# Two more Strassen pairs in each of four feed-forward blocks, and the sums they read as a task of their own

## The chip, the core and the metric

The kernel runs on one core of one Trainium2 chip. What counts is the device time of one execution, in microseconds (us). The four engines that matter here are PE (TensorE, matmuls and transpositions), DVE (VectorE), ACT (ScalarE) and POOL (GpSimd); SP issues the loads. Each engine works through its own instructions in a fixed order.

## The reference

Two stacked blocks on a sequence of 512 rows with 1024 features. What is touched here is the SwiGLU feed-forward layer (inner width 2816), which stands four times in the first part of the model, each time followed by a scaled residual and a LayerNorm:

```python
def swiglu_ffn(x, wi, wo):
    gate, up = jnp.split(x @ wi, 2, axis=-1)
    return (jax.nn.silu(gate) * up) @ wo
```

All of it is in float32. Mixers of several kinds, attention and two further feed-forward blocks stand between and behind; the change does not touch their code.

## The kernel before, in words

**Precision.** A float32 product is made of three matmuls of a shorter type: each operand is split into a high part (`xh`, `wh`, made by ACT as a rounded copy) and a low part (`xl`, `wl`, made by DVE as the difference), and PE adds `wh.xh + wh.xl + wl.xh` (`mm3`; its matmuls are all on line 319 of the profile, transpositions on line 324). Operations of the other engines go through a wrapper and all show line 55, so they are told apart by their tiles.

**A feed-forward block** (`ffn_block1`, called four times: blocks 1 to 4 below). The 22 pairs of gate and up slabs of 128 columns go in three parts of 6, 8 and 8 pairs (`PARTS`); after each part a down-projection (`down`, tile `mg` in the first part) adds what the part gives. The four products of pairs 0 and 1 are made by `gemm_first`, tile `mf`, k by k while x is being completed. A *plain* pair from then on is two products of 8 k-steps x 3 matmuls of 512 columns, tile `m`: 48 matmuls. After a pair, ACT makes the sigmoid part `sg`, DVE `hf`, ACT `hh`, DVE `hl` (`unit`).

**A Strassen pair** (class `Fast`, weights in class `Pair`). A pair's product is a 2 x 2 block product: the two weight slabs by the two halves of the inner dimension, against the halves of x's features and of its columns. In the Winograd form it takes seven products of half the size instead of eight: A11, S2, A12, S3, S1, A22, S4, in that order, each 4 k-steps x 3 matmuls of 256 columns, 84 matmuls. A11 and A12 read x itself; S4's product reads x too; S2, S3, S1 and A22 read four *combinations* T1 to T4 of x. The weights S1 to S4 are sums of raw slabs (`ws`, `wr`) that DVE makes. The low parts of S1 and S2 do not go over DVE: ACT writes minus the high part, and a DMA of GpSimd's queue adds the raw value (`wl<-ws`). The results are put together on DVE from the parts of PSUM.

**The combinations** (class `Combos`). First the eight sums `ys[k] = xh + xl` (tiles `y`, 128x512, DVE); from these, in four steps of k, two tiles `ta` and `tb` by four DVE operations of 256 columns; ACT's `th` and DVE's `tl` split each. The `y` are later also the accumulators of the down-projection.

**The order of the work.** `Sched` holds a model of the engines' times while the program is written out: tasks (generators) are kept in a list with due times, and `wait`, `upto` and `pump` run them where they are due. A task yields a due time (`pace`: not over 2 us ahead of DVE), or a condition. The compiler's scheduler then also sets the order in which each engine's instructions stand. That order, once built, is fixed: an engine does not pass an operation that waits.

**Before the change**, which pairs are Strassen pairs is the tuple `FAST`: pairs 4 to 7, 9, 10, 12 to 15, 17, 18, 20, 21. The eight sums are emitted behind `gemm_first` and the first units, and the combinations are then a task (`cb.make`). Pairs 2 and 3 are plain. Block 1 starts with `load_start`: x is read in eight pieces, transposed by PE (tile `xT`) in two halves of k, and split, all before the first matmul of `gemm_first`.

Of the kernel before, what the change touches and what calls it, by code (L numbers as in the profile page):

```python
# [14 lines left out]
ALU = mybir.AluOpType  # L15
AX = mybir.AxisListType
PSUM = bass.MemoryType.PSUM
P = 128
NT = 512
KD = 8  # L20
# [499 lines left out]
HALF = (slice(0, 256), slice(256, 512))  # L520
ALPHA = 4.0 ** 0.25
PARTS = ((0, 6), (6, 8), (14, 8))
FAST = (4, 5, 6, 7, 9, 10, 12, 13, 14, 15, 17, 18, 20, 21)
RAW1, HL1 = 6, 7


# [72 lines left out]
def load_start(g, x, X0, n=4):  # L599

    g.preload(AF.Silu)
    ts, raw = {}, {}
    for hf in range(2):
        for t in range(4):
            a = ts[t, hf] = g.f("xs")
            g.nc.sync.dma_start(a, x[t * P:(t + 1) * P, hf * NT:(hf + 1) * NT])
        for j in range(n):
            a = raw[j, hf] = g.f("wr")
            g.wq[j][0](a.rearrange("p (k c) -> p k c", k=4), 4 * hf, 4)
    for j in range(n):  # L610
        g.whl_t[j] = []
    for hf in range(2):
        for o in range(4):
            k = 4 * hf + o
            ps = g.psum("xT")
            for t in range(4):
                g.tr(ps[:, t * P:(t + 1) * P], ts[t, hf][:, o * P:(o + 1) * P])
            g.split_x(X0.h[k], X0.l[k], ps)
        for j in range(n):
            hi, lo = g.f("wh", F32R), g.f("wl", F32R)  # L620
            g.split_x(hi, lo, raw[j, hf])
            g.whl_t[j] += [(hi[:, k * P:k * P + P], lo[:, k * P:k * P + P]) for k in range(4)]
    g.wi_dma = g.wi_hi = g.wi_split = n
    X0.ready = [KD, KD]


def gemm_first(g, xs, n, by_half=True):

    w = [g.slab(0) for _ in range(n)]
    g.acq_main(n)  # L630
    ps = [g.psum("mf") for _ in range(n)]
    for hf, c in enumerate(HALF if by_half else (slice(0, NT),)):
        for k in range(KD):
            g.s.wait(lambda: xs.ready[hf] > k)
            g.s.upto(*xs(k), w[0][k][1])
            for j in range(n):
                g.mm3(ps[j][:, c], w[j][k], xs(k, c), k == 0, k == KD - 1)
            if k % 2 and (hf or not by_half):
                g.split_ahead()
            g.s.pump()  # L640
    g.slab_done(n)
    return ps
# [107 lines left out]
def down(g, xs_of, kt):  # L750

    yield from head(g, xs_of, kt, 2)
    for m in range(2, KD):
        yield m, gemm_tile(g, xs_of, kt)
# [60 lines left out]
class Combos:  # L815
# [3 lines left out]
    def __init__(self, g, xs, ys):  # L819
        self.g, self.xs, self.ys = g, xs, ys  # L820
        self.t = {}
        self.n = 0

    def make(self):
        g = self.g
        TT = g.nc.vector.tensor_tensor
        a, b = HALF
        for k in range(4):
            lo, hi = self.ys[k], self.ys[4 + k]
            s, u = g.f("ta"), g.f("tb")  # L830
            TT(s[:, a], lo[:, b], lo[:, a], ALU.subtract)
            TT(s[:, b], hi[:, b], s[:, a], ALU.subtract)
            yield g.pace()
            TT(u[:, a], hi[:, b], lo[:, b], ALU.subtract)
            TT(u[:, b], hi[:, a], s[:, b], ALU.subtract)
            yield g.pace()
            for nm, t in (("s", s), ("u", u)):
                h, l = g.f("th", F32R), g.f("tl", F32R)
                g.split_x(h, l, t)
                self.t[nm, k] = (h, l)  # L840
            self.n = k + 1
            yield g.pace()
        self.ys = None
# [71 lines left out]
            g.rel()  # L915


def ffn_block1(g, xs, gv, bv, hook=None, into=None, by_half=True, fast=()):

    nc = g.nc  # L920
    ys = [g.f("y") for _ in range(KD)]
    st = Stats(g, True)
    pipe = Pipe()
    for pi, (k0, n) in enumerate(PARTS):
        hs = {}

        def unit(j, pg, pu):
            sg, hf = g.f("sg"), g.f("hf")
            nc.scalar.activation(sg, pg(), AF.Silu)
            g.rel()  # L930
            yield True
            nc.vector.scalar_tensor_tensor(hf, sg, 0.5, pu(), ALU.mult, ALU.mult)
            g.rel()
            hh, hl = g.f("hh", F32R), g.f("hl", F32R)
            nc.scalar.activation(hh, hf, AF.Copy)
            yield True
            nc.vector.tensor_tensor(hl, hf, hh, ALU.subtract)
            hs[j] = (hh, hl)

        def unit_fast(j, e):  # L940
            sg, hf = e.c1, e.c2
            nc.scalar.activation(sg, sg, AF.Silu)
            yield True
            nc.vector.scalar_tensor_tensor(hf, sg, 0.5, hf, ALU.mult, ALU.mult)
            hh, hl = g.f("hh", F32R), g.f("hl", F32R)
            nc.scalar.activation(hh, hf, AF.Copy)
            yield True
            nc.vector.tensor_tensor(hl, hf, hh, ALU.subtract)
            hs[j] = (hh, hl)

        j = k0
        if pi == 0:
            ps = gemm_first(g, xs, 4, by_half)
            for i in range(2):
                pipe.add(unit(i, lambda: ps[2 * i], lambda: ps[2 * i + 1]))
                pipe.step()
            j = 2
            for k in range(KD):
                nc.vector.tensor_tensor(ys[k], xs.h[k], xs.l[k], ALU.add)
            g.raw_lim, g.hl_lim, g.ahead = RAW1, HL1, 2  # L960
            cb = Combos(g, xs, ys)
            if fast:
                g.s.spawn(cb.make())
        open_ = {}
        for j, nm in pair_order(range(j, k0 + n), fast):
            if nm is None:
                ps = [gemm_tile(g, xs)]
                pipe.add(unit(j, lambda: ps[0], lambda: ps[1]))
                ps.append(gemm_tile(g, xs))
                pipe.step()  # L970
                continue
            g.s.wait(lambda: cb.n == 4)
            if j not in open_:
                open_[j] = Fast(g, cb)
            e = open_[j]
            e.step(nm)
            if nm == "S4":
                pipe.add(unit_fast(j, e))
                del open_[j]
        pipe.drain()  # L980
        if pi == len(PARTS) - 1:
            g.raw_lim, g.ahead = 0, 1
        of = lambda k, c=slice(0, NT): (hs[k0 + k][0][:, c], hs[k0 + k][1][:, c])
        if pi == 0:
            for m, ps in down(g, of, n):
                nc.vector.scalar_tensor_tensor(ys[m], ys[m], ALPHA, ps, ALU.mult, ALU.add)
                g.rel()
        elif pi == 1:
            for m, ps in down(g, of, n):
                nc.vector.tensor_tensor(ys[m], ys[m], ps, ALU.add)  # L990
                g.rel()
        else:
            xn = []

            def evac(m, ps, c):
                nc.vector.tensor_tensor(ys[m][:, c], ys[m][:, c], ps, ALU.add)

            def finish(hf):
                if not xn:
                    xn.append(into() if into else X(g, "x"))  # L1000
                if into:
                    return xn[0].ln_half(st, ys, hf, gv, bv)
                return ln_half(g, st, ys, hf, gv, bv, xn[0])

            out_proj_ln(g, ys, of, n, 4, evac, st, finish, head(g, of, n, 2))
        if hook and pi == 0:
            hook()
    return xn[0]
# [1877 lines left out]
def kernel(ctx: ExitStack, tc: tile.TileContext, d, out: bass.AP):  # L2886
    g = G(ctx, tc)
    x0 = X(g, "x")
# [17 lines left out]
    def first_setups():  # L2906
        yield lambda: g.vec_done
        setup_even(g, d)
        yield 20000.0
        setup_blk2(g, d)  # L2910

    plan_ffn(g, d["ffn1_wi"][0], d["ffn1_wo"][0], fast=FAST)
    plan_even(g, d["ev_w_in"][0], d["ev_w_out"][0])
    plan_ffn(g, d["ffn2_wi"][0], d["ffn2_wo"][0], fast=FAST)
    plan_ffn(g, d["ffn1_wi"][1], d["ffn1_wo"][1], fast=FAST)
    plan_odd(g, d["od_w_in"][0], d["od_w_out"][0], lambda l: plan_mem(g, d["w_mem_kv_2"][l]))
    plan_ffn(g, d["ffn2_wi"][1], d["ffn2_wo"][1], fast=FAST)
    for l in range(2):
        plan_attn(g, d, l)
        plan_ffn2(g, d, l)  # L2920
    load_start(g, d["x"][0], x0)

    ln = lambda l, i: (v[f"ln_g{l}{i}"], v[f"ln_b{l}{i}"])
    def man(n):
# [5 lines left out]
        return tc.manual_schedule(engines=e) if e != set() else contextlib.nullcontext()  # L2930

    with man("f"):
        x = ffn_block1(g, x0, *ln(0, 0), hook=lambda: g.s.spawn(first_setups()), by_half=False, fast=FAST)
    with man("even"):
        x = even_block(g, x, d, *ln(0, 1))
    with man("f"):
        x = ffn_block1(g, x, *ln(0, 2), fast=FAST)
        x = ffn_block1(g, x, *ln(1, 0), hook=lambda: setup_odd(g, d), fast=FAST)
    mkv, mhl = [], ([], [])
    with man("odd"):  # L2940
        x = odd_block(g, x, d, *ln(1, 1), mem_norm(g, d["mem_2"][0], v["mem_norm_g"], *mhl),
                      lambda l: mkv.append(mem_kv(g, *mhl)))
    g.hl_bufs = HB1
    with man("f3"):
        rx = ffn_block1(g, x, *ln(1, 2),
                            into=lambda: RX(g, [g.f("x") for _ in range(KD)], v["g_pre_mix0"]), fast=FAST)
# [42 lines left out]
```

## Time and profile before

| what | value |
|---|---|
| times of three runs | 3631.16, 3628.79, 3620.95 us (median 3628.79) |
| the profiled execution's own time | 3618.88 us |
| its span, first to last instruction | 3616.9 us |
| mean granted TensorE clock | 0.991 |
| PE busy | 3548.0 us, 98% of the span, 21720 instructions |
| DVE busy | 2412.3 us, 67% |
| ACT busy | 1641.5 us, 45% |
| POOL busy | 423.0 us, 12% |

The time is that of a whole execution, the span that of its instructions. A row of the timeline gives the start, the busy time, engine, line, operation, output and inputs with their shapes, and in brackets the idle time before it and what ended it. The first row of a run of n like operations shows the busy time of all n. A matmul's own duration contains the part in which the next already runs, so the pitch from one to the next is the cost.

### The profile page before, as it was taken

The numbers are of one execution on the slowest core, as the hardware profiler recorded it, in microseconds if no ns is written. First come the engines' busy times: TensorE is split into PE (matmuls) and PEld (weight loads), VectorE is DVE, ScalarE is ACT, GpSimd is POOL, SyncE is SP. The second block draws the span as 40 slices with busy tenths as digits, with TensorE's granted clock in tenths as the row PEclk, the third lists the DMA queues.
The fourth block names the chain that finished last, engine by engine and source line by source line (L and its number), as shares of the span: only waits on it lengthen the run. The fifth ranks groups of instructions, "written<-read, shape, count | busy, mean of one in ns | idle before, by whom it ended". The sixth has DMA issues, their size and how long they took to land.

```text
span 3616.9 us, 57977 instructions
## 1 busy us (share of the span) xinstructions
PE 3548.0 (98%) x21720; PEld 3024.1 (84%) x21720; DVE 2412.3 (67%) x4499; ACT 1641.5 (45%) x3169; POOL 423.0 (12%) x615
## 2 busy tenths in 40 slices
PE   9999999999999999988999999999999999999999
PEld 7889868898989997667888988788888987888888
DVE  6666968775776577776865675557656745467755
ACT  5444764444444456533543454435434444354433
POOL 0102003000210021011100210021000110120001
PEclk9999999999999999998999999999999999999999
DMA  5555322454445441113354533232333252333331
GB/s 150 132 128 124 88 59 81 107 135 117 110 120 129 112 106 48 37 53 88 85 132 122 124 116 110 88 111 62 106 101 93 75 153 73 96 88 104 92 90 53
DMA packets 631243, 361.52 MB, mean 100 GB/s; under 512 B 27025, under 2 KB 609842, under 8 KB 630962
## 3 DMA queue, kind: packets, MB, share of 16 engines
q1 hardware_dynamic: 612018, 324.81, 31.2%
q0 software_dynamic: 16128, 29.37, 5.0%
q8 instruction: 170, 2.79, 0.3%
q10 hardware_dynamic: 2816, 3.64, 0.3%
q14 instruction: 111, 0.91, 0.1%
HBM read 323.65 MB, written 4.74 MB: 91 GB/s over the span
## 4 chain that ended last, share of the span: by engine, by line
PE 45%; DVE 3%; issue 1%; DMA 1%; ACT 1%; POOL 0%; DVEq 0%; ACTq 0%; POOLq 0%
PE m L319 33%; PE mg L319 3%; PE mf L319 2%; PE tk L319 2%; PE br L319 2%; PE mh L319 1%; DVE rm_t L55 0%; DMA wl<-ws 0%; PE naS L319 0%; PE naO L319 0%; PE dO L319 0%; DVE x L55 0%; PE naT L324 0%; PE st L319 0%; DVE xgl L55 0%
## 5 line engine op out<-in xcount | busy, mean ns | idle before, releaser
L55 DVE TENSOR_TENSOR wl<-wr,wh 128x512 fp32r<-128x512 f32 (+2 forms) x1264 | 864.9, 724 | 236.7 <-ACT wh L55 213.5
L55 ACT ACTIVATE wh<-wr 128x512 fp32r<-128x512 f32 (+2 forms) x1264 | 696.4, 608 | 118.6 <-PE m L319 44.5
L319 PE MATMUL m<-xgh,wh 128*128 128x512 f32 x1184 | 471.2, 398 | 1.2 <-DVE dmx L55 1.2
L319 PE MATMUL m<-xgh,wl 128*128 128x512 f32 x1184 | 467.2, 395 | 0.0
L319 PE MATMUL m<-xgl,wh 128*128 128x512 f32 x1184 | 467.2, 395 | 0.0
L319 PE MATMUL m<-xh,wh 128*128 128x512 f32 (+1 forms) x1320 | 455.4, 345 | 0.1
L319 PE MATMUL m<-xh,wl 128*128 128x512 f32 (+1 forms) x1320 | 446.8, 339 | 2.9 <-DVE wl L55 2.9
L319 PE MATMUL m<-xl,wh 128*128 128x512 f32 (+1 forms) x1320 | 446.3, 338 | 0.0
L319 PEld LDWEIGHTS m<-xh,wh 128*128 128x128 f32 x1320 | 249.4, 189 | 38.2 <-issue 8.4
L319 PEld LDWEIGHTS m<-xh,wl 128*128 128x128 f32 x1320 | 249.6, 189 | 32.9 <-DVE wl L55 4.0
L319 PEld LDWEIGHTS m<-xl,wh 128*128 128x128 f32 x1320 | 249.8, 189 | 28.9 <-issue 1.7
L319 PEld LDWEIGHTS m<-xgh,wh 128*128 128x128 f32 x1184 | 222.7, 188 | 57.1 <-issue 4.8
L319 PEld LDWEIGHTS m<-xgh,wl 128*128 128x128 f32 x1184 | 222.7, 188 | 52.3 <-issue 0.2
L319 PEld LDWEIGHTS m<-xgl,wh 128*128 128x128 f32 x1184 | 222.8, 188 | 50.2 <-issue 0.2
L319 PE MATMUL m<-th,wl 128*128 128x256 f32 x896 | 252.3, 282 | 6.5 <-DMA wl<-ws 6.3
L319 PE MATMUL m<-tl,wh 128*128 128x256 f32 x896 | 251.0, 281 | 0.0
L319 PE MATMUL m<-th,wh 128*128 128x256 f32 x896 | 250.1, 281 | 0.0
L319 PE MATMUL m<-hh,wh 128*128 128x512 f32 x600 | 236.5, 394 | 0.0
L319 PE MATMUL m<-hl,wh 128*128 128x512 f32 x600 | 236.4, 394 | 0.0
L319 PE MATMUL m<-hh,wl 128*128 128x512 f32 x600 | 236.2, 394 | 0.0
L55 POOL DMA_DIRECT2D wl<-ws x112 | 96.2, 859 | 1109.6 <-ACT wl L55 781.7
L319 PEld LDWEIGHTS m<-th,wl 128*128 128x128 f32 x896 | 168.6, 188 | 8.3 <-DMA wl<-ws 8.1
(577 smaller groups left out, 7484.4 us busy)
## 6 DMA issues: line engine op xcount, KB each, us to landing
wr<-in_ffn_wi_dram SPq DMA_DIRECT2D x352, 256.0 KB
wr<-in_w_up_dram SPq DMA_DIRECT2D x176, 256.0 KB
wr<-in_ffn_wo_dram SPq DMA_DIRECT2D x160, 256.0 KB
wr<-in_w_in_dram SPq DMA_DIRECT2D x152, 256.0 KB
wl<-ws POOLq DMA_DIRECT2D x112, 256.0 KB, 3.9
wr<-in_w_down_dram SPq DMA_DIRECT2D x80, 256.0 KB
wr<-in_od_w_in_dram SPq DMA_DIRECT2D x50, 256.0 KB
wr<-in_ev_w_in_dram SPq DMA_DIRECT2D x48, 256.0 KB
```

The source lines that it names most:

```text
L55: r = fn(*a, **kw)
L319: return self.nc.tensor.matmul(out, lhsT, rhs, start=start, stop=stop, **kw)
```

## The change

1. `FAST` has 16 pairs instead of 14: pairs 2 and 3 are added, and in the second part 7 to 10 take the place of 6, 7, 9, 10 (pair 8 in, pair 6 out). It holds for all four blocks.
2. The eight sums are the beginning of a new task, `Combos.sums`, which is started ahead of `gemm_first`, waits until x is complete, writes the sums one by one at DVE's pace, and goes on with `make`.
3. `load_start` transposes and splits only the first half of x, and returns a function for the second half; `gemm_first` calls that in block 1 at k = 2.
4. Ahead of the first down-projection stands a wait in the emission, until all four combinations are written.

The first lines of the diff that say so:

```diff
-FAST = (4, 5, 6, 7, 9, 10, 12, 13, 14, 15, 17, 18, 20, 21)
+FAST = (2, 3, 4, 5, 7, 8, 9, 10, 12, 13, 14, 15, 17, 18, 20, 21)
...
-    for hf in range(2):
+
+    def half(hf):
         for o in range(4):
             k = 4 * hf + o
             ps = g.psum("xT")
...
-            g.whl_t[j] += [(hi[:, k * P:k * P + P], lo[:, k * P:k * P + P]) for k in range(4)]
+            parts[j] += [(hi[:, k * P:k * P + P], lo[:, k * P:k * P + P]) for k in range(4)]
+        X0.ready = [4 + 4 * hf] * 2
...
-    X0.ready = [KD, KD]
+    half(0)
+    return lambda: half(1)
...
         for k in range(KD):
+            if second and k == 2:
+                second()
             g.s.wait(lambda: xs.ready[hf] > k)
...
+    def sums(self):
+
+        g, xs, ys = self.g, self.xs, self.ys
+        yield lambda: min(xs.ready) == KD
+        for k in range(KD):
+            g.nc.vector.tensor_tensor(ys[k], xs.h[k], xs.l[k], ALU.add)
+            yield g.pace()
+        yield from self.make()
...
         if pi == 0:
-            ps = gemm_first(g, xs, 4, by_half)
+            cb = Combos(g, xs, ys)
+            if fast:
+                g.s.spawn(cb.sums())
+            ps = gemm_first(g, xs, 4, by_half, second)
...
-            for k in range(KD):
-                nc.vector.tensor_tensor(ys[k], xs.h[k], xs.l[k], ALU.add)
             g.raw_lim, g.hl_lim, g.ahead = RAW1, HL1, 2
-            cb = Combos(g, xs, ys)
-            if fast:
-                g.s.spawn(cb.make())
...
         if pi == 0:
+            g.s.wait(lambda: cb.n == 4)
             for m, ps in down(g, of, n):
```

The built program has 19666 instructions on PE instead of 19378 (36 more for each of eight pairs), 4468 instead of 4380 on DVE, 3023 instead of 2975 on ACT, 16 more on POOL, and as many on SP.

**DVE, block 2, behind the first product.** Before, the two `hf` (which read `mf` and the sigmoid `sg`) come first, then the sums and the combinations, with weights' low parts and the next units between:

```order
L55 SCALAR_TENSOR_TENSOR hf_6719<-sg_6718,mf_6414 128x512
L55 TENSOR_TENSOR hl_6723<-hf_6719,hh_6722 128x512
L55 SCALAR_TENSOR_TENSOR hf_6727<-sg_6726,mf_6416 128x512
L55 TENSOR_TENSOR y_6403<-xh_6224,xl_6232 128x512
...
L55 TENSOR_TENSOR y_6410<-xh_6231,xl_6239 128x512
L55 TENSOR_TENSOR ta_6746<-y_6403 128x256
L55 TENSOR_TENSOR hl_6731<-hf_6727,hh_6730 128x512
L55 TENSOR_TENSOR ta_6746<-y_6407,ta_6746 128x256
L55 TENSOR_TENSOR wl_6780<-wr_6640,wh_6778 128x512
```

Now the last of four sums stands ahead of the first `hf`, four stand behind the second, and the four steps of combinations follow without a break; weights' low parts come behind the last `tl`:

```order
L55 TENSOR_TENSOR y_6534<-xh_6355,xl_6363 128x512
L55 TENSOR_TENSOR wr_6228<-wr_6228,ws_6724 128x512
L55 SCALAR_TENSOR_TENSOR hf_6829<-sg_6828,mf_6542 128x512
L55 TENSOR_TENSOR hl_6833<-hf_6829,hh_6832 128x512
L55 SCALAR_TENSOR_TENSOR hf_6837<-sg_6836,mf_6544 128x512
L55 TENSOR_TENSOR y_6535<-xh_6356,xl_6364 128x512
...
L55 TENSOR_TENSOR ta_6847<-y_6531 128x256
L55 TENSOR_TENSOR tb_6848<-y_6535,y_6531 128x256
L55 TENSOR_TENSOR ta_6847<-y_6535,ta_6847 128x256
L55 TENSOR_TENSOR tb_6848<-y_6535,ta_6847 128x256
L55 TENSOR_TENSOR tl_6854<-ta_6847,th_6853 128x512
...
L55 TENSOR_TENSOR tl_6900<-tb_6890,th_6899 128x512
```

Blocks 3 and 4 read alike, with seven sums ahead of the first `hf` in block 3.

**PE, block 2, behind the first product.** Before, the first product is followed by a plain pair:

```order
L319 MATMUL mf_6416<-xl_6239,wh_6092 128x256
L319 MATMUL mf_6416<-xh_6231,wl_6096 128x256
L319 MATMUL m_6745<-xl_6232,wh_6591 128x512
L319 MATMUL m_6745<-xh_6224,wl_6595 128x512
L319 MATMUL m_6745<-xh_6225,wh_6591 128x512
```

Now it is followed by A11 (tile `m_6903`) and A12 (`m_6965`) of pair 2, 12 matmuls each, of which the last two stand first here; then S2 and S3 alternate, six matmuls for each step of the combinations; then two of S1 (`m_7010`), whose third reads the low part that comes by DMA:

```order
L319 MATMUL m_6965<-xl_6367,wh_6761 128x256
L319 MATMUL m_6965<-xh_6359,wl_6794 128x256
L319 MATMUL m_6903<-th_6853,wh_6727 128x256
L319 MATMUL m_6965<-th_6857,wh_6797 128x256
L319 MATMUL m_6903<-tl_6854,wh_6727 128x256
...
L319 MATMUL m_6965<-th_6899,wl_6825 128x256
L319 MATMUL m_7010<-th_6853,wh_6916 128x256
L319 MATMUL m_7010<-tl_6854,wh_6916 128x256
L319 MATMUL m_7048<-xh_6356,wh_6926 128x256
```

Seven further matmuls (six of S4, one of A11 of pair 3) stand between these and S1's third.

**DVE, block 1.** The second half of x (`xl_97` to `xl_100`) stood right behind the first product's first four low parts; now four operations on pair 2's weights stand ahead of it:

```order
L55 TENSOR_TENSOR wl_177<-wr_118,wh_176 128x512
L55 TENSOR_TENSOR wl_228<-wr_190,wh_226 128x512
L55 TENSOR_TENSOR ws_230<-wr_192,wr_194 128x512
L55 TENSOR_TENSOR ws_231<-ws_230,wr_190 128x512
L55 TENSOR_TENSOR wr_192<-wr_190,wr_192 128x512
L55 TENSOR_TENSOR xl_97<-xT_236,xh_89 128x512
```

Before, `xl_97` stood directly behind `wl_177`.

## Rows read from the trace of the kernel before

**Rows 1.** The core's span and its mean granted clock.
```profile
core 0: 3616.9 us, clock 0.991
```

**Rows 2.** Windows: length, PE, PEld, DVE, ACT, POOL busy (x), PEclk, DMA, GB/s.
```profile
992.00:1014.30 22.30, 22.30 (x98) 18.09 (x98) 18.37 (x33) 10.53 (x19) 1.74 (x2) 1.00 0.23 53
1014.30:1036.70 22.40, 20.68 (x169) 20.00 (x168) 20.43 (x42) 13.05 (x26) 1.72 (x2) 1.00 0.41 101
15.90:39.10 23.20, 23.20 (x98) 18.80 (x97) 9.38 (x15) 9.63 (x17) 0.00 (x0) 1.00 0.71 186
```

**Rows 3.** The chain that ended last: start, length, what.
```profile
1790.84 4.77 DMA wl<-ws
...
2480.78 18.97 PE mf L319 x160
...
2667.50 11.15 PE mg L319 x48
```

**Rows 4.** PE's waits: in total, times, longest.
```profile
PE m L319 <- DMA wl<-ws: 6.3, 7, 1.7
```

**Rows 5.** Timeline of DVE in block 3, behind the first product.
```profile
993.05 0.69 DVE L55 SCALAR_TENSOR_TENSOR hf<-sg,mf 128x512 f32<-128x512 f32 x1 [2.44 <-ACT sg L55]
...
995.64 4.90 DVE L55 TENSOR_TENSOR y<-xh,xl 128x512 f32<-128x512 f32 x8
...
1015.01 0.42 DVE L55 TENSOR_TENSOR ta<-y 128x256 f32<-128x256 f32 x1
...
1018.01 0.42 DVE L55 TENSOR_TENSOR ta<-y 128x256 f32<-128x256 f32 x1
```

**Rows 6.** Timeline of DVE: the first hf of blocks 2 and 4.
```profile
634.60 0.69 DVE L55 SCALAR_TENSOR_TENSOR hf<-sg,mf 128x512 f32<-128x512 f32 x1 [2.31 <-ACT sg L55]
...
1754.92 0.69 DVE L55 SCALAR_TENSOR_TENSOR hf<-sg,mf 128x512 f32<-128x512 f32 x1 [1.24 <-ACT sg L55]
```

**Rows 7.** S1's lo slab in block 3 (ACT, PE), and the page's row of such DMAs.
```profile
1025.01 0.62 ACT L55 ACTIVATE wl<-ws 128x512 fp32r<-128x512 f32 x1
...
1029.84 0.39 PE L319 MATMUL m<-th,wl 128*128 128x256 f32 x1 [1.47 <-DMA wl<-ws]
...
wl<-ws POOLq DMA_DIRECT2D x112, 256.0 KB, 3.9
```

**Rows 8.** Timeline of PE: the first down-projection's first matmul, blocks 1 to 4.
```profile
84.18 0.39 PE L319 MATMUL mg<-hh,wh 128*128 128x512 f32 x1
...
679.68 0.39 PE L319 MATMUL mg<-hh,wh 128*128 128x512 f32 x1
...
1036.75 0.40 PE L319 MATMUL mg<-hh,wh 128*128 128x512 f32 x1
...
1799.80 0.39 PE L319 MATMUL mg<-hh,wh 128*128 128x512 f32 x1
```

**Rows 9.** Timeline of PE, DVE and ACT in block 1's start.
```profile
10.94 2.49 DVE L55 TENSOR_TENSOR wl<-wr,wh 128x512 fp32r<-128x512 f32 x4
...
16.45 0.63 PE L319 MATMUL mf<-xl,wh 128*128 128x512 f32 x1
...
17.73 0.48 PE L319 MATMUL mf<-xl,wh 128*128 128x512 f32 x1
...
21.24 1.36 ACT L55 ACTIVATE wh<-wr 128x512 fp32r<-128x512 f32 x2 [0.20 <-DMA wr<-in_ffn_wi_dram]
...
41.18 1.28 ACT L55 ACT_TABLE_LOAD   x1
```

**Rows 10.** Windows, columns as in rows 2: PE's load in one, its clock in the next.
```profile
1550.50:1553.90 3.40, 1.21 (x4) 0.30 (x2) 3.22 (x6) 2.45 (x5) 1.23 (x1) 1.00 0.47 143
1553.90:1557.30 3.40, 3.33 (x8) 2.68 (x9) 3.40 (x9) 0.00 (x0) 0.00 (x0) 0.50 0.04 12
...
1717.70:1721.10 3.40, 1.70 (x15) 1.49 (x13) 1.82 (x4) 0.75 (x2) 3.24 (x4) 1.00 0.48 142
1721.20:1724.60 3.40, 1.99 (x11) 1.54 (x12) 1.10 (x4) 0.80 (x2) 2.45 (x4) 1.00 0.04 12
```

More of the change, by code (lines that the diff above doesn't have):

```diff
@@ L601, in load_start @@
     g.preload(AF.Silu)
-    ts, raw = {}, {}
+    ts, raw, parts = {}, {}, [[] for _ in range(n)]
     for hf in range(2):
@@ L609, in load_start @@
             g.wq[j][0](a.rearrange("p (k c) -> p k c", k=4), 4 * hf, 4)
-    for j in range(n):
-        g.whl_t[j] = []
-    for hf in range(2):
+    def half(hf):
         for o in range(4):
@@ L621, in load_start, with gemm_first @@
             g.split_x(hi, lo, raw[j, hf])
-            g.whl_t[j] += [(hi[:, k * P:k * P + P], lo[:, k * P:k * P + P]) for k in range(4)]
+            parts[j] += [(hi[:, k * P:k * P + P], lo[:, k * P:k * P + P]) for k in range(4)]
+        X0.ready = [4 + 4 * hf] * 2
+    for j in range(n):
+        g.whl_t[j] = parts[j]
     g.wi_dma = g.wi_hi = g.wi_split = n
-    X0.ready = [KD, KD]
-def gemm_first(g, xs, n, by_half=True):
+    half(0)
+    return lambda: half(1)
+def gemm_first(g, xs, n, by_half=True, second=None):
     w = [g.slab(0) for _ in range(n)]
@@ L915, in step, with ffn_block1 @@
             g.rel()
-def ffn_block1(g, xs, gv, bv, hook=None, into=None, by_half=True, fast=()):
+def ffn_block1(g, xs, gv, bv, hook=None, into=None, by_half=True, fast=(), second=None):
     nc = g.nc
@@ L2920 @@
         plan_ffn2(g, d, l)
-    load_start(g, d["x"][0], x0)
+    second = load_start(g, d["x"][0], x0)
     ln = lambda l, i: (v[f"ln_g{l}{i}"], v[f"ln_b{l}{i}"])
@@ L2932 @@
     with man("f"):
-        x = ffn_block1(g, x0, *ln(0, 0), hook=lambda: g.s.spawn(first_setups()), by_half=False, fast=FAST)
+        x = ffn_block1(g, x0, *ln(0, 0), hook=lambda: g.s.spawn(first_setups()), by_half=False, fast=FAST, second=second)
     with man("even"):
```

## The prediction

> **What bounds the kernel now.** I read the profile from the whole inwards. The granted clock over the span is 0.991 and PE is busy for 98% of it [rows 1], so the time falls only where PE has less to do, and rises wherever PE is made to wait. Next, the windows of the third feed-forward block's first part [rows 2]: in 992.00 to 1014.30, while PE works through two plain pairs, PE is busy 22.30 of 22.30 us and DVE 18.37; in 1014.30 to 1036.70, with two Strassen pairs, PE is busy 20.68 of 22.40 and DVE 20.43. So PE sets the pace, but DVE has only 4 us to spare in the first stretch, and 2 in the second. Then the chain of work that ended last, for the pitch of a matmul [rows 3]: 48 of 512 columns in 11.15 us (0.232 each), 160 of 256 columns in 18.97 us (0.118 each). PE's list of waits [rows 4] shows how little the old order lost at the DMA that finishes a Strassen slab: 6.3 us in 7 waits.
>
> **What the edit is worth on PE alone.** A plain pair is 48 matmuls x 0.232 = 11.1 us, a Strassen pair 84 x 0.118 = 9.9 us: 1.2 less. Two more such pairs in four blocks are 8 x 1.2 = 9.6 us less. This is the gain, if nothing makes PE wait.
>
> **What the plain pairs 2 and 3 covered.** S2, S3, S1 and A22 read the activations' combinations th and tl, which need DVE for eight sums y, sixteen ta/tb and eight tl. Before, all of that ran beside two plain pairs (22.3 us of full PE, [rows 2]). In the changed order PE goes from the last matmul of the first product straight to pair 2: A11 and A12 (24 matmuls, 2.8 us) need no combination; the next, S2 and S3, wait for the first one. The wait is set by DVE's order in the new listing: in blocks 2 and 4 four sums stand ahead of the first unit's hf and four behind it, in block 3 seven and one, and all four steps of combinations stand behind the two hf and the hl between them. hf waits for the sigmoid of the first product's result, which is read when that product has ended. So the sums' task, although it begins earlier, doesn't get the combinations earlier than the end of the first product: the four steps are queued behind an operation that waits for PE.
>
> Lengths on DVE [rows 5]: from the start of the first hf to the end of the second is 2.6 us (993.05 to 995.64, where the next operation begins); eight sums are 4.90 us, 0.61 each; a step of the combinations is 3.0 us (ta at 1015.01, the next step's ta at 1018.01). The first hf began at 634.60 in block 2 and at 1754.92 in block 4 [rows 6]; in block 3 at 993.05 [rows 5], behind 2.44 us in which DVE had nothing. Seven sums there take 4.3, so hf comes up to 1.8 later, less where a sum finds an earlier gap: I take 1.1, 994.2. The last tl then ends at
> - block 2: 634.6 + 2.6 + 4 x 0.61 + 4 x 3.0 = 651.6
> - block 3: 994.2 + 2.6 + 0.61 + 12.0 = 1009.4
> - block 4: 1754.9 + 2.6 + 2.4 + 12.0 = 1771.9
>
> **The second wait, S1.** ACT's new order puts S1's wh and wl behind the eighth th, so its DMA (lo part accumulated on GpSimd's queue) can only be asked for at the end of the steps. In block 3, ACT's wl began at 1025.01 and lasted 0.62; the first matmul that reads it began at 1029.84, after a wait for that DMA [rows 7]: 4.2 us from the wl's end. The longest of these DMAs in the chain took 4.77 [rows 3], the median of all is 3.9 from issue to landing [rows 7]. I take 4.2, the same operation in the same place, with the other two as bounds. With 0.2 for the wl itself, S1 can begin 4.4 us after the last tl. In between PE has nine matmuls; behind it are 28 of pair 2 (22 of S1 and A22, 6 of S4; 3.3 us), and then pairs 3 to 5, 3 x 9.9 = 29.8 us, as steady Strassen work: DVE's 20.43 us in the second window [rows 2] hold two such pairs and at least two steps of the combinations (6.0), so a pair costs it 7.2 us or, by my count of its operations, up to 8.9: under PE's 9.9. So the first matmul of the first down-projection comes 4.4 + 3.3 + 29.8 = 37.5 us behind the last tl: 689.1, 1046.9, 1809.4. Before, it came at 679.68, 1036.75, 1799.80 [rows 8]. **Blocks 2 to 4: +9.4, +10.2, +9.6, together +29.2.** The saved 2.4 us of each block and the old waits for S1 are inside these differences, since they are made from end to end.
>
> **Block 1.** Here the halves of x's transposition help. The first product began at about 15.9 (PE is full in the window from there, [rows 2]) and at half pitch (0.43 a matmul, three from 16.45 to 17.73, where [rows 3] give 0.23; [rows 9]). With the first half's transpositions alone ahead of it, it can begin at about 10.9, where DVE has done four xl and begins the first wl; 24 matmuls, the other 16 transpositions, then 72 matmuls (16.7 us). The second half's xl now stand on DVE behind four operations of pair 2, whose raw slabs were still landing: the first for which ACT waited came at 21.24, and one came in each 0.9 us, so I put the four at 17.7 to 20.4. The product then ends at about 36.6 to 37, 20.2 + 16.7, where it ended at 39.1 [rows 2]: 2.5 us gained. But only the first step of the combinations is ordered ahead of hf (which begins then). Behind it come hf, hl, hf and the constants' copies and set-up (2.6 + 1.4), three steps (9.0) and a table load on ACT between the th (1.28, [rows 9]): the last tl ends at about 50.7. S1 follows 4.4 later, then 34 matmuls and the vectors' transpositions (4.9), then 29.8: 89.8 against 84.18 [rows 8]. **Block 1: +5.6.**
>
> **The clock.** Where PE was busy for 1.21 of 3.40 us, the next stretch of the same length was granted 0.50, that is 1.2 GHz; after 1.70 of 3.40 it was still granted 1.00, 2.4 GHz [rows 10]. In the new stall PE has nothing at all between A12 and the first step (5 to 6 us), and then 12 matmuls in each step of 3.0 us (1.42 us), between those two rows. While it waits, a lower clock costs nothing; what runs behind S1's arrival at 1.2 GHz costs double. I take 10 matmuls of these, 1.2 us a block, 5 in all; the bounds are 0, and the whole 28 (3.3 us a block, 13 in all). The Trainium skill, page "TensorE: Matmul & The Clock Gate", section "HAM oscillation — how this bites in real kernels", says that idle gaps put PE back to half rate, and that this happens anew in every loop step that waits. By that rule the clock stays low in each of the four stalls and the whole of what follows S1 in pair 2 is slow: 8 us more than my sum. [Rows 10] show the fall, and none of them shows how a row of short bursts fares.
>
> Parts 2 and 3 of the blocks keep their number of Strassen pairs; pairs 7 to 10 now stand four in a row, which DVE holds (7 to 9 against 9.9). I cost that at nothing; without DVE's cover it would be some tenths a pair. The new wait before the first down-projection is passed long before. DMAs stay as many on SP; POOL gets 16 more.
>
> **Sum.** 29.2 + 5.6 + 5 = **+40 us**. The profiled execution took 3618.88 us against a median of 3628.79 for the runs (3620.95 to 3631.16), so it lies below all three: the sum gives 3659 on its own time and 3669 on the median. I forecast **3665**. About 0.3% (11 us) is what a measurement of this kernel can tell from no change.
>
> **Rivals.**
> *The clock outlasts the stall.* If the clock stays at 1.2 GHz through S1 to S4 of pair 2 and half of pair 3, each block costs 3.3 + 5 instead of 1.2: 7 more, 28 in all, +68, 3690 or over. For it: the bursts lie near the row that lost the clock. Against: behind S1 PE is fully busy, and after the half rate at the very start the window from 15.90 on still has a mean granted clock of 1.00 [rows 2]. Chance 0.06.
> *Half a stall.* A step of the combinations may be shorter than 3.0, as the one I measured has ACT's th in between: its six operations at their pitch are 4 x 0.33 + 2 x 0.61 = 2.5. That, S1's DMA at 3.9 and the clock unharmed give 40 - 8 - 1 - 5 = +26; with a larger gain in block 1 (first product at full clock at once, and combinations ahead of hf) +15 to +20: about 3635 to 3650. Chance 0.12.
> *The gain is only eaten up.* Stall and gain cancel if the last tl comes 9 us sooner than I put it, 6 us behind the first hf instead of 15 to 17: 3629. It needs the steps to be half done before hf, in all blocks, where the listing has that only in part for block 1. Chance 0.06.
> *Faster.* If DVE reaches the combinations while PE still has A11 and A12, within 2.8 us of the end of the first product, there is no stall: -9.6, the old waits for S1 (-6.3, [rows 4]) and -2.5 at the start, 3611. It decides at that point, a tl of the first step by about 995 in block 3, and the rest at 1.4 us a step. For it: DVE is not at its limit before hf. Against it: its operations stand in a fixed order behind hf, which waits for PE, and a step took twice that. Chance 0.04.
>
> **How the numbers follow.** The forecast's case, a stall of some 10 us in each of blocks 2 to 4 and some 6 in block 1 (+26 to +58), has 0.72. Its low end is the shorter steps, the shorter DMA and no loss of clock (+26, on the profiled execution's time 3645); its high end is a DMA of 4.8, the whole of 28 matmuls at 1.2 GHz and steps of 3.5, which is 40 + 2 + 8 + 8 = +58, on the median 3687. The range's ends are these, rounded outwards. So 3640 to 3688 takes this case and part of the half stall. Faster by over 0.3%: 0.04. Within 0.3%: 0.06. Slower: 0.72 + 0.12 + 0.06 = 0.90.
>
> **What would show it.** In the profile after: S2's and S3's first matmuls waiting some 5 us for DVE's tl or ACT's th, then a wait of about 2 us in each of the next three steps; S1's first matmul waiting 3 us for the DMA; th, tl and S1 at the head of PE's waits with 10 to 15 us a block; the first down-projection at 89.8, and later by some 10 us in each block that follows; PE's share down to about 97%. I am wrong if th and tl of the first step end before the first product does, if PE's busy share stays at 98% with a shorter span, or if the stall is there and a later stretch gives the time back.

## The result and the profile after

The changed kernel took 3669.19 us (median of three runs, 3667.23 to 3676.55) against 3628.79: the ratio of the runs is 1.0131, with a 95% interval of 1.0114 to 1.0148. It is slower by 1.3%, and the forecast of 3665 with its range of 3640 to 3688 held. The two medians alone give 1.011 and 40 us. The later comparisons timed the kernel before again, 11 to 15 runs each, with medians of 3623.0 to 3623.6; the mean of all its 44 runs is 3623.7, that of the changed kernel's three 3671.0, which agrees with the ratio. So the change costs some 47 us and not 40. The profiled execution took 3669.19 us, 50 more than that of before.

PE's list of waits in the profile after (time in all, times, longest), beside [rows 4]:

```profile
PE m L319 <- ACT th L55: 24.9, 16, 4.9
PE m L319 <- DMA wl<-ws: 12.3, 8, 4.0
```

The first row is new: 16 waits for the combinations, four in each block. The second has doubled. The first matmul of the first down-projection, in the four blocks, beside [rows 8]:

```profile
94.54 0.40 PE L319 MATMUL mg<-hh,wh 128*128 128x512 f32 x1
...
703.50 0.39 PE L319 MATMUL mg<-hh,wh 128*128 128x512 f32 x1
...
1074.19 0.39 PE L319 MATMUL mg<-hh,wh 128*128 128x512 f32 x1
...
1847.30 0.40 PE L319 MATMUL mg<-hh,wh 128*128 128x512 f32 x1
```

Block 1 is 10.4 us late (94.54 against 84.18). For the others the start of the first product has to be taken off; it came at 610.66, 967.36 and 1731.30 before and at 622.16, 991.05 and 1766.46 after. From there to these rows it was 69.0, 69.4 and 68.5 us before and is now 81.3, 83.1 and 80.8: 12.3, 13.8 and 12.3 more. That is 48.8 us of the 50.6 by which the span grew (3616.9 to 3667.5); all else together is 1.8, of which the second part, where pair 8 took the place of pair 6, has 1.4 in the four blocks. So the loss sits where it was forecast, in four places. DVE in block 2, behind the first product, beside [rows 5, 6]:

```profile
646.27 0.69 DVE L55 SCALAR_TENSOR_TENSOR hf<-sg,mf 128x512 f32<-128x512 f32 x1 [0.15 <-ACT sg L55]
...
648.86 2.49 DVE L55 TENSOR_TENSOR y<-xh,xl 128x512 f32<-128x512 f32 x4
651.27 0.42 DVE L55 TENSOR_TENSOR ta<-y 128x256 f32<-128x256 f32 x1
...
654.27 0.42 DVE L55 TENSOR_TENSOR ta<-y 128x256 f32<-128x256 f32 x1
...
662.65 0.69 DVE L55 TENSOR_TENSOR tl<-tb,th 128x512 fp32r<-128x512 f32 x1
664.12 1.90 DVE L55 TENSOR_TENSOR wl<-wr,wh 128x512 fp32r<-128x512 f32 x3 [0.79 <-ACT wh L55]
```

The first hf waits for the sigmoid, four sums follow the second hf, the steps are 3.0 us apart, and the last tl ends at 663.3: 17.1 us behind hf's start. PE at the same place:

```profile
649.23 0.28 PE L319 MATMUL m<-xh,wl 128*128 128x256 f32 x1
653.08 1.10 PE L319 MATMUL m<-th,wh 128*128 128x256 f32 x2 [3.57 <-ACT th L55]
...
662.06 1.10 PE L319 MATMUL m<-th,wh 128*128 128x256 f32 x2 [0.87 <-ACT th L55]
...
668.77 0.58 PE L319 MATMUL m<-th,wl 128*128 128x256 f32 x1 [2.08 <-DMA wl<-ws]
```

A12's last matmul starts at 649.23; then PE waits for each step, and at 668.77 for S1's low part. Its clock meanwhile (windows, columns as in rows 2):

```profile
651.00:654.00 3.00, 0.92 (x3) 0.69 (x4) 2.73 (x7) 1.15 (x2) 0.00 (x0) 0.64 0.00 0
654.00:657.00 3.00, 2.12 (x8) 1.50 (x8) 2.73 (x7) 1.15 (x2) 0.00 (x0) 0.50 0.00 0
...
666.00:669.00 3.00, 0.92 (x5) 0.62 (x4) 2.15 (x5) 1.42 (x3) 0.00 (x0) 0.50 0.67 139
669.00:672.00 3.00, 3.00 (x15) 3.00 (x16) 1.96 (x4) 2.34 (x5) 1.71 (x2) 0.50 0.72 164
672.00:675.00 3.00, 3.00 (x26) 3.00 (x26) 1.75 (x4) 0.36 (x1) 0.00 (x0) 0.95 0.73 145
```

The granted clock falls to 0.50 in the first gap, stays there through the steps and S1's wait, and reads 0.95 in the window from 672.00, PE having been full since 668.77. What the low clock costs behind S1 can be read from the starts of the matmuls there:

```profile
671.93 0.41 PE L319 MATMUL m<-tl,wh 128*128 128x256 f32 x1
672.14 0.36 PE L319 MATMUL m<-th,wl 128*128 128x256 f32 x1
672.34 0.28 PE L319 MATMUL m<-th,wh 128*128 128x256 f32 x1
672.46 0.28 PE L319 MATMUL m<-tl,wh 128*128 128x256 f32 x1
```

Up to 672.34 they stand 0.21 us apart, from then on 0.12. The 16 matmuls from 668.77 to 672.34 took 3.6 us where 16 at full pitch take 1.9: 1.7 us. In blocks 1, 3 and 4 it was 22, 27 and 15 such matmuls and 2.3, 2.7 and 1.6 us. The windows behind S1 in those blocks:

```profile
56.30:58.30 2.00, 2.00 (x9) 2.00 (x10) 1.30 (x4) 2.00 (x5) 0.85 (x1) 0.50 0.33 98
1038.50:1041.50 3.00, 3.00 (x14) 3.00 (x15) 1.96 (x4) 2.54 (x5) 1.55 (x2) 0.50 0.60 143
1812.50:1815.00 2.50, 2.50 (x12) 2.50 (x13) 1.38 (x4) 2.50 (x6) 0.86 (x1) 0.50 0.57 156
```

In the steps themselves DVE is busy for 2.73 of every 3.00 us: the whole stretch goes at DVE's pace.

### The profile page after: what moved, and what is told of

Same layout as the page of the kernel before. It is cut to its first block, busy times and chain, and to the rows that moved or that the text cites. A ratio compares the mean times of both kernels' runs of the same rounds, so it can differ in the third digit from the quotient of the medians.

```text
span 3667.5 us, 58814 instructions
## 1 busy us (share of the span) xinstructions
PE 3567.4 (97%) x22008; PEld 3051.7 (83%) x22008; DVE 2454.7 (67%) x4587; ACT 1665.7 (45%) x3217; POOL 438.3 (12%) x631
## 4 chain that ended last, share of the span: by engine, by line
PE 83%; DVE 9%; issue 3%; ACT 3%; DMA 2%; POOL 1%; SPq 0%; DVEq 0%; ACTq 0%; POOLq 0%
PE m L319 58%; PE mg L319 5%; PE mf L319 4%; PE mh L319 3%; PE tk L319 3%; PE br L319 2%; DVE wl L55 1%; DVE ln_z L55 1%; DMA wl<-ws 1%; DVE y L55 1%; DVE rst L55 1%; ACT wh L55 1%; ACT L55 0%; PE st L319 0%; DVE rm_t L55 0%
## 5 line engine op out<-in xcount | busy, mean ns | idle before, releaser
L319 PE MATMUL m<-xh,wh 128*128 128x256 f32 (+1 forms) x1288 | 432.8, 336 | 1.1 <-ACT wh L55 1.0
L319 PE MATMUL m<-xh,wl 128*128 128x256 f32 (+1 forms) x1288 | 423.6, 329 | 2.5 <-DVE wl L55 2.5
L319 PE MATMUL m<-xl,wh 128*128 128x256 f32 (+1 forms) x1288 | 423.1, 329 | 0.0
L319 PE MATMUL m<-th,wh 128*128 128x256 f32 x1024 | 298.6, 293 | 25.1 <-ACT th L55 24.9
L319 PE MATMUL m<-th,wl 128*128 128x256 f32 x1024 | 296.5, 290 | 12.3 <-DMA wl<-ws 12.3
L319 PE MATMUL m<-tl,wh 128*128 128x256 f32 x1024 | 297.5, 291 | 0.1
L319 PEld LDWEIGHTS m<-xgl,wh 128*128 128x128 f32 x1184 | 223.0, 188 | 50.6 <-issue 0.2
L55 POOL DMA_DIRECT2D wl<-ws x128 | 110.2, 861 | 1118.7 <-ACT wl L55 828.4
L319 PEld LDWEIGHTS m<-th,wh 128*128 128x128 f32 x1024 | 199.4, 195 | 32.4 <-ACT th L55 32.4
```

Of the source, the lines that this page charges most:

```text
L55: r = fn(*a, **kw)
L319: return self.nc.tensor.matmul(out, lhsT, rhs, start=start, stop=stop, **kw)
```

## The experiments

Each was compared with the kernel before on the same chip. The changed kernel's ratio, 1.0131, is the mark for all; stages are read in the profiled executions.

**e1, the old pairs.** The sums' task and the halves stay:

```diff
-FAST = (2, 3, 4, 5, 7, 8, 9, 10, 12, 13, 14, 15, 17, 18, 20, 21)
+FAST = (4, 5, 6, 7, 9, 10, 12, 13, 14, 15, 17, 18, 20, 21)
```

> The changed kernel with the old 14 pairs: sums as a task and the first transpositions in halves stay, pairs 2 and 3 are plain again. Theory (the stall comes with Strassen's form at pair 2, whose combinations no plain pair covers): the waits of PE for th are gone, the first down-projection of blocks 2 to 4 comes 68.5 to 69.4 us after the first product's start as before, block 1 gains 2 to 3 us at the start; in all 2 to 5 us under the kernel before, which the runs can hardly tell from none. Rival (the sums' task or the halves cost the time themselves, by their place ahead of hf): 10 to 40 us over the kernel before.

3614.39 us, ratio 0.9983 (0.9967 to 0.9999). The waits for th are gone. The stages from the first product to the down-projection take 68.5, 67.6 and 68.5 us in blocks 2 to 4, and block 1's ends at 82.25. The rival falls: the task and the halves cost nothing by themselves, and the loss comes with the pairs: some 54 us from this run to the changed kernel, by the two ratios.

**e2, the pairs alone.** The kernel before, with the new `FAST` and nothing else.

> The kernel before with the 16 pairs alone: no task for the sums, no halves. Theory: the same stall, and longer, since all eight sums stand behind the second hf: four sums (2.4 us) more in blocks 2 and 4, seven (4.2, less 1 to 2 of a later hf) in block 3, and in block 1 the later start; 8 to 15 us slower than the changed kernel, 50 to 60 over the kernel before. Rival (task and halves cost the time): within 10 us of the kernel before.

3685.96 us, ratio 1.0175 (1.016 to 1.019), 62 us over the kernel before and 16 over the changed kernel, a little more than expected. DVE in block 2 shows why it is worse than the changed kernel:

```profile
650.01 0.69 DVE L55 SCALAR_TENSOR_TENSOR hf<-sg,mf 128x512 f32<-128x512 f32 x1 [2.60 <-ACT sg L55]
...
652.66 4.90 DVE L55 TENSOR_TENSOR y<-xh,xl 128x512 f32<-128x512 f32 x8
```

All eight sums stand behind hf, and DVE waits 2.60 us in front of it. The sums' task does what it says; together with the halves it takes some 16 us off a loss that the pairs bring.

**e3, pair 2 plain, from pair 3 on.**

```diff
-FAST = (2, 3, 4, 5, 7, 8, 9, 10, 12, 13, 14, 15, 17, 18, 20, 21)
+FAST = (3, 4, 5, 7, 8, 9, 10, 12, 13, 14, 15, 17, 18, 20, 21)
```

> The changed kernel with pair 2 plain (15 of 22, from pair 3 on). The listing puts the combinations behind the hf of pair 2, which waits for that pair's second product. Theory (what sets the stall is the DVE operation that waits for PE and stands ahead of the combinations): the stall moves to pair 3 and stays: PE waits for th again, for the first step some 2 us less than in the changed kernel, S1's low part is asked for earlier and its wait goes; the first down-projection some 3 us later than before in each of blocks 2 to 4, so 5 to 14 us over the kernel before. Rival (only the length of the combinations from the end of the first product counts, some 17 us, of which a plain pair with A11 and A12 covers 14): 10 to 18 us under the kernel before.

3642.26 us, ratio 1.0055 (1.0039 to 1.0072): 19 over the kernel before, where the rival had it 10 to 18 under. The theory's sign was right and its size (5 to 14) too small: the first down-projection came 6 to 7 us late in blocks 2 to 4, not 3. DVE in block 2, and PE's wait at the second step (at the first it was 0.2 us):

```profile
649.28 0.69 DVE L55 SCALAR_TENSOR_TENSOR hf<-sg,m 128x512 f32<-128x512 f32 x1 [1.98 <-PE m L319]
649.88 0.68 DVE L55 TENSOR_TENSOR y<-xh,xl 128x512 f32<-128x512 f32 x1
650.49 0.42 DVE L55 TENSOR_TENSOR ta<-y 128x256 f32<-128x256 f32 x1
```

```profile
655.35 1.02 PE L319 MATMUL m<-th,wh 128*128 128x256 f32 x3 [1.23 <-ACT th L55]
```

The combinations now stand behind the hf of pair 2 (its input is `m`), which DVE waits for. One plain pair ahead doesn't cover them here, where an operation of that same pair stands ahead of them; how it would do without that, no run shows.

**e4, the combinations ahead of hf.**

```diff
             ps = gemm_first(g, xs, 4, by_half, second)
+            g.s.wait(lambda: cb.n == 4)
             for i in range(2):
```

> The changed kernel with one line more: the units of pairs 0 and 1 (sigmoid, hf, hl) are written after all four steps of the combinations, so that on DVE nothing that waits for the first product stands ahead of them. Theory: the two hf and the hl (2.6 us) and the wait for the sigmoid go from ahead of the last tl, so it ends some 3 us sooner in each of blocks 2 to 4 and some 4 in block 1, but the twelve us of the steps stay uncovered: 10 to 16 us faster than the changed kernel, still 25 to 38 over the kernel before. Rival (the queue behind hf is the whole cause of the stall): within 10 us of the kernel before.

3673.85 us, ratio 1.0141 (1.0126 to 1.0156): no faster than the changed kernel, and both readings miss. What was asked for did happen: the last tl comes 38.1 us after the first product's start in block 2, where it was 41.2. But ACT then shows this:

```profile
658.13 1.28 ACT L55 ACT_TABLE_LOAD   x1
659.42 0.60 ACT L55 ACTIVATE sg<-mf 128x512 f32<-128x512 f32 x1
660.78 0.63 ACT L55 ACTIVATE hh<-hf 128x512 fp32r<-128x512 f32 x1 [0.76 <-DVE hf L55]
661.31 0.58 ACT L55 ACTIVATE sg<-mf 128x512 f32<-128x512 f32 x1
662.76 0.63 ACT L55 ACTIVATE hh<-hf 128x512 fp32r<-128x512 f32 x1 [0.87 <-DVE hf L55]
663.29 0.61 ACT L55 ACTIVATE wh<-ws 128x512 fp32r<-128x512 f32 x1
```

S1's wh stands behind the table load, both sigmoids and both hh, and PE's waits have a new first row:

```profile
PE m L319 <- ACT wh L55: 21.3, 8, 5.2
PE m L319 <- ACT th L55: 14.0, 14, 1.4
```

Counted from the first product's start in block 2, the last tl ends 3.0 us sooner than in the changed kernel, S1's wh starts 2.2 us later (42.5 against 40.3), and the first down-projection comes at 81.8 against 81.3. So the units, moved behind the combinations, delay the next weights by most of what they had delayed the combinations. Taking all that waits for the first product from ahead of the combinations was not enough: the wait for hf is a part of the stall and not the whole.

**e5, PE kept at work.** Additional matmuls, whose results are overwritten, ahead of each step of S2 in pair 2:

```diff
+            if self.fill and nm == "S2":
+                self.keep(10 if k else 28, w[0], self.cb("S2", k - 1) if k else self.cb("A11", 0))
             x = self.cb(nm, k)
```

> The changed kernel with additional matmuls into a bank whose content is overwritten later, 28 ahead of the first step of pair 2's S2 and 10 in each of the next three steps, in each block, all in stretches in which PE waited: they keep PE at work while it waits for the combinations. Theory (the clock that falls to 1.2 GHz in the stall costs what runs behind S1's arrival, 34.7 to 35.7 us to the first down-projection against 33.1 at full pitch): granted clock at 1.00 through the stall, and 1.6 to 3 us less in each block, 6 to 12 faster than the changed kernel. Rival (the low clock is hidden by the waits and costs nothing): within 3 us of the changed kernel. Rival (the low clock costs the whole of what stands behind the stall in pair 2, and more): 13 us or more faster.

3672.81 us, ratio 1.0137 (1.0122 to 1.0153): as the changed kernel. Windows of block 2:

```profile
654.00:657.00 3.00, 2.17 (x16) 1.96 (x16) 2.73 (x6) 1.16 (x3) 0.00 (x0) 1.00 0.00 0
657.00:660.00 3.00, 2.17 (x16) 1.96 (x16) 2.73 (x6) 1.16 (x3) 0.00 (x0) 1.00 0.00 0
660.00:663.00 3.00, 2.19 (x10) 1.51 (x10) 2.19 (x4) 3.00 (x6) 0.86 (x1) 1.00 0.12 35
663.00:666.00 3.00, 1.66 (x7) 1.11 (x5) 3.00 (x6) 0.80 (x3) 0.00 (x0) 0.57 0.96 230
666.00:669.00 3.00, 1.76 (x8) 1.76 (x9) 1.86 (x5) 3.00 (x7) 0.85 (x1) 0.50 0.17 25
```

The clock stays at 1.00 through the steps, as meant, and falls in S1's wait instead, which was not filled. So the matmuls behind S1 ran at 1.2 GHz just the same: from S1's start at 667.24 to the down-projection at 701.60 it took 34.4 us, in the changed kernel 34.7. The run doesn't remove the low clock behind S1; what it costs there is in the pitch shown above. It shows that in front of S1 the low clock cost nothing: from the first product's start to the end of the last tl block 2 took 41.2 us with either clock.

**e6, S1's weights ahead too.** As e4, with

```diff
+            g.raw_lim, g.hl_lim, g.ahead = RAW1, HL1, 2
+            g.split_ahead(3)
             g.s.wait(lambda: cb.n == 4)
```

> As e4_combos_first, and the weights of S1, A22 and S4 of pair 2 are split ahead of the combinations too, so that S1's high and low part no longer stand on ACT behind the sigmoid and hh. Theory (each engine's queue hands the stall on: in e4 the 3 us gained on DVE were lost in front of S1 on ACT): PE's waits for S1's wh and its DMA in pair 2 go, but the next sum of weights, S2 of pair 3, is made behind the hf on DVE, goes over ACT and the DMA, and is there about 12 to 13 us after the last tl, where PE wants it after 7: 2 to 4 us a block are left as gain, 8 to 16 faster than the changed kernel. Rival (S1's queue on ACT was the last obstacle): 20 us or more faster than the changed kernel.

3669.74 us, ratio 1.0128 (1.0114 to 1.0142): no gain, where the theory had 8 to 16 us and named S2 of pair 3. The waits behind the combinations moved on, but to nearer work, A11 of pair 3:

```profile
667.15 0.39 PE L319 MATMUL m<-xh,wh 128*128 128x256 f32 x1 [3.17 <-ACT wh L55]
```

Its wh is the next thing on ACT behind the two hh. That the stall would be handed on to the next queue came out again; the place that I named did not.

**e7, S1's low part on DVE.**

```diff
-            if isinstance(self.wq[j][0], Pair) and self.wq[j][1] in Pair.BY_DMA:
+            if isinstance(self.wq[j][0], Pair) and self.wq[j][1] in self.wq[j][0].by_dma:
...
-                    pairs[j] = Pair(g, w_a, j * P, 2816 + j * P)
+                    pairs[j] = Pair(g, w_a, j * P, 2816 + j * P, ("S2",) if j == 2 else Pair.BY_DMA)
```

> The changed kernel with the low part of S1 of pair 2 made by DVE instead of ACT and the DMA. Theory of the prediction (the second wait, S1's DMA, 4.3 to 5.5 us behind the last tl, stands on the path by itself): S1 begins 1 us behind the last tl, and 3.5 to 4.5 us a block go, 14 to 18 faster than the changed kernel. Rival (behind it stands S2 of pair 3, whose DMA lands about 11 us behind the last tl): half of it at most, 4 to 9 us faster than the changed kernel, with a new wait of PE for that DMA.

3659.16 us, ratio 1.0100 (1.0086 to 1.0113), that is 11 us under the changed kernel by the two ratios: between the two expectations. DVE splits S1 right behind the last tl:

```profile
659.70 0.68 DVE L55 TENSOR_TENSOR tl<-tb,th 128x512 fp32r<-128x512 f32 x1
660.30 0.68 DVE L55 TENSOR_TENSOR wl<-ws,wh 128x512 fp32r<-128x512 f32 x1
```

From the end of the last tl to the down-projection block 2 took 36.4 us instead of 40.2, blocks 1, 3 and 4 took 39.4, 37.1 and 37.4 instead of 43.5, 41.2 and 39.1: 13.7 us in all. PE's waits for such DMAs fell from 12.3 to 7.0 us. The rival's new wait, for S2 of pair 3, came up in blocks 1, 3 and 4, at 0.9, 1.0 and 0.7 us, which took back a part of the gain but no more. S1's DMA was on the path by itself. No run put this together with e4 or e6.

**e8, one more wait taken off e1.** S2 of pair 5 split on DVE, in the same way as in e7.

> e1_old_fast (the changed kernel with the old 14 pairs), and the low part of S2 of pair 5, for whose DMA PE still waits 1 to 1.4 us in each block, made by DVE. Theory: DVE has room for one operation of 0.6 us there; these waits go, 4 to 6 us faster than e1_old_fast, 9 to 12 under the kernel before. Rival (DVE is the bound in this stretch, 20.4 of 22.4 us busy before): no gain over e1_old_fast, or a loss of 1 to 3 us.

3619.42 us, ratio 0.9989 (0.9981 to 0.9998): no gain over e1. The row of these DMAs in PE's waits reads 6.7 us in 5 waits against 5.6 in 7; the waits moved to S1 of that pair (3.2 us in block 2).

**e9 to e11, where Strassen's form pays.** e1 with pair 8 added; e1 with all pairs from 4 on; and the kernel before with the halves alone.

```diff
+FAST = (4, 5, 6, 7, 8, 9, 10, 12, 13, 14, 15, 17, 18, 20, 21)
...
+FAST = (4, 5, 6, 7, 8, 9, 10, 11, 12, 13, 14, 15, 16, 17, 18, 19, 20, 21)
```

> e1_old_fast with one pair more in Strassen's form, pair 8 in the second part, where the combinations have long been there (15 of 22). Theory (the form itself gives 1.2 us a pair wherever DVE is not the bound; only at pairs 2 and 3 it has no combinations yet): 4 x 1.2 = 4.8 us under e1_old_fast, 9 to 11 under the kernel before. Rival (a Strassen pair more costs DVE, ACT or the DMA what PE saves): no faster than e1_old_fast.

> e1_old_fast with all pairs from 4 on in Strassen's form (18 of 22: 8, 11, 16 and 19 besides). Theory: 16 x 1.2 = 19 us under e1_old_fast, 22 to 26 under the kernel before, as DVE was busy for 66% of parts 2 and 3 and a Strassen pair costs it 5.3 us more than a plain one (to about 72%). Rival (in a long row of such pairs DVE's 8.9 of 9.9 us a pair leave too little, waits for ACT, DVE or the DMA come up at every pair): within 8 us of e1_old_fast.

> The kernel before with the first transpositions in halves alone: no task for the sums, the old 14 pairs. Theory: block 1's first product starts 4 to 5 us earlier and ends 2 us earlier, the first down-projection there comes about 2 us earlier than 84.18, and nothing else moves: 2 us under the kernel before, which no run can tell from none. Rival (the sums' task gives the rest of what e1_old_fast showed): the same here, and the 2 to 4 us that e1_old_fast gained in blocks 2 to 4 are missing.

e9: 3610.35 us, ratio 0.9964 (0.9952 to 0.9977). e10: 3603.07 us, ratio 0.9947 (0.9933 to 0.9961): 20 us under the kernel before, 66 under the changed one. It beats both. Windows inside the second part of block 2, 80 us of e1 and then 90 us of e10:

```profile
695.00:775.00 80.00, 80.00 (x516) 72.47 (x515) 51.61 (x91) 34.87 (x66) 8.59 (x10) 1.00 0.53 126
```

```profile
685.00:775.00 90.00, 90.00 (x671) 85.69 (x671) 68.21 (x125) 44.98 (x85) 12.58 (x15) 1.00 0.57 135
```

DVE goes from 65% busy to 76% and PE stays full. The stages from one down-projection to the next shrank from 115.3 and 126.3 us (e1) to 113.1 and 125.5 there, 3.0 us for four pairs; in the four blocks it is 15.4 for sixteen, about 1.0 a pair where 1.2 was expected. By the ratios e10 gained 13 us on e1 and e9 gained 7, each uncertain by several us. For e9 the stages give 5.7, the theory's 5 rather than none; for e10 it lies between the theory's 19 and the rival's 8, and the 15.4 of the stages are nearer to the theory.

e11: 3626.95 us, ratio 1.001 (1.0 to 1.0019). The first product starts at 10.91, as expected, but the first down-projection comes at 86.16, 2 us later than before instead of 2 sooner: the wait for pair 5's S2 grew from 1.4 to 2.9 us, and 2.5 us more were lost behind it. That was the clock, as two windows from there on show:

```profile
76.70:79.70 3.00, 3.00 (x14) 3.00 (x15) 1.24 (x3) 1.07 (x3) 0.00 (x0) 0.50 0.28 79
82.70:85.70 3.00, 3.00 (x28) 3.00 (x27) 1.54 (x4) 0.00 (x0) 0.00 (x0) 1.00 0.33 98
```

In the kernel before, the same wait of 1.4 us left the clock at 1.00. Without the sums' task the earlier start is worth nothing.

## Why the prediction was right

The place, the sign and the row of waits were right, and the forecast total lies within 5 us of the median. That closeness is in part luck: the steps' sum was 9 us short of the profile's, and the base was high. Of the cause, the prediction had only a part. By the steps of the prediction:

| step | forecast | measured |
|---|---|---|
| first hf to last tl, blocks 2, 3, 4 | 17.0, 15.2, 17.0 | 17.1, 15.3, 17.1 |
| last tl to S1's first use of the low part, blocks 1 to 4 | 4.4 | 5.2, 5.4, 5.5, 4.3 |
| from there to the down-projection, blocks 2 to 4 | 33.1, and 1.2 for the clock | 34.7, 35.7, 34.8 |
| the same in block 1 | 34.7, and 1.2 | 38.3 |
| later first down-projection, block 1 | 5.6, and 1.2 | 10.4 |
| blocks 2, 3, 4 | 9.4, 10.2, 9.6, and 1.2 each | 12.3, 13.8, 12.3 |
| all blocks together | 40 | 48.8 |

The queue behind hf in blocks 2 to 4 was read to a tenth of a microsecond: a fixed order and durations from the same operations leave little to guess. In block 1 two misses nearly cancel: the first hf began at 37.8 and not at 36.6, and from there to the end of the last tl it took 13.2 us. My terms for that add up to 14.3, so they give an end at 50.9 where I wrote 50.7; it was 51.05. One count in the prediction is wrong: a step of the combinations feeds six matmuls, three of S2 and three of S3, and not 12. At full pitch that is 0.7 us and not 1.42, less than in either of the rows [rows 10] between which I put the stall. PE's waits were 3.6 to 4.9 us for the first step in blocks 2 to 4 and 0.9 for each of the next, where I had said some 5 and 2; at the low clock the six matmuls, which start as th and tl come, stretch over 2.1 of the 3.0 us.

Three terms were too small. **S1's DMA**: from the end of ACT's wl (663.57) to the first matmul it was 5.2 us in block 2 and not 4.2, and over the four blocks that step was 2.9 us longer than 4 x 4.4. The row I took the 4.2 from, [rows 7], is that of S2 of pair 5 and not of S1, as its heading and the prediction have it: the same operation, DMA and wait, in another place. **The clock behind S1**: I took 10 matmuls at 1.2 GHz and 1.2 us a block; it was 15 to 27 matmuls and 1.6 to 2.7 us, 8.3 in all where I had 5. That is nearly all of what the tails of blocks 2 to 4 took over 33.1. In block 1 another wait of 1.2 us for such a DMA (in pair 4) stands besides. **Block 4's hf**, which came 1.0 later than I put it.

The rule of the Trainium skill (page "TensorE: Matmul & The Clock Gate", section "HAM oscillation — how this bites in real kernels"), idle gaps that put PE back to half rate anew each time, is what the windows show in all four stalls. By it I had put the tails at 8 us more than my sum, with all 28 matmuls behind S1 slow; what was slow cost 3.3 us more than my sum, 27 of the 28 in block 3 and fewer elsewhere. In front of S1 the low clock cost nothing, as e5's filled steps show.

Why the total still came out at 3669 against 3665: the three runs of before that I took the base from lie about 5 us above the kernel's later medians, which made up for a part of the 9 us that the steps' sum was short; and the forecast stands 4 below the 3669 of my sum on the median.

Of the rivals, the clock that outlasts the stall into pair 3 didn't come: in every block it was back within pair 2, in block 3 only at its last matmuls. The half stall fell with the steps, 3.0 and not 2.5. The gain that is eaten up, and the faster case, fell with the order on DVE.

What e4 and e6 add is that the prediction's picture of the cause was too narrow. I wrote that the combinations are held up by hf; taken from behind hf, the loss stayed as large, at the next weights. Behind the first product lie the units, the sums, the combinations and two pairs' weights, for DVE and ACT; in the old order two plain pairs, 22.3 us of full PE, are the time in which this is done ([rows 2]: DVE 18.37 of 22.30). In each of the three orders run (the changed kernel, e4, e6), what was put behind came late instead.

## What to carry to other kernels

A form of the product that saves PE work is worth having only where the engines that prepare it have time: with all else as in e1, two more such pairs in each block cost some 54 us at the start of the blocks, and four others in each gained some 13 further on, where what they read had long been there. Before moving a consumer forward, list all that its producers' engines must do between its new place and the last thing they wait for; if that is longer than the cover, another order may only hand the loss on, as in e4 and e6. What did help was work done earlier, while the first product ran (the sums' task with the halves, 16 us against e2), and a shorter way for the last piece (S1's low part on DVE, 11 us in e7). And look in that list for an operation that itself waits for the slow engine (a plain pair's hf in e3): it can undo the cover.

## What the runs showed of the hardware

In the steps of the changed kernel PE worked in bursts between its waits, and the granted clock stayed at 0.50 (1.2 GHz) through all of them; in e5 the same steps with the fill had 1.00, and the clock fell to 0.50 in the wait that was not filled. Behind the stall a matmul of 256 columns stood 0.21 us from the next at 0.50 and 0.12 at 1.00.

Profiled executions differ in a stretch that no experiment touched. The odd mixer between blocks 3 and 4, with the same order of PE's instructions, took 401.4 us in e1 and 413.3 in e11 (from its first product to that of block 4). PE's waits were 2.4 us longer in e11; most of the rest is in stretches in which PE went without a wait in both, at the slower pitch in e11 and not in e1. In one window of 100 us near the middle the clock was 1.00 in e1 and 0.93 in e11:

```profile
1427.00:1527.00 100.00, 98.16 (x1225) 70.47 (x1227) 79.01 (x224) 55.29 (x101) 2.16 (x5) 1.00 0.13 34
```

```profile
1432.00:1532.00 100.00, 98.51 (x1135) 70.69 (x1137) 73.98 (x213) 51.30 (x94) 0.41 (x4) 0.93 0.13 34
```

A difference of 10 us between two profiled executions of this kernel must be looked for stage by stage before it is put down to a change; that is why the table above goes by stages.
